# Two FFN projections of a hybrid decoder trunk as seven half-size block products instead of eight

## Chip, cores and metric

One NeuronCore of a Trainium2 chip. The metric is the device time of one execution in microseconds (us), the median of three runs.

## The reference

A decoder trunk of two layers on x of 1024 positions by 1024 features, float32. Layer 0 mixes with a state-space model and gated linear attention, layer 1 with an xLSTM matrix memory. After each mixer, and after each feed-forward block, the result is normalised and added to x. What the change concerns is the feed-forward block (FFN) that stands behind each mixer:

```python
def conv_ffn(h, w_up, conv_w, conv_b, w_down):          # h: 1024 x 1024
    g, u = jnp.split(h @ w_up, 2, axis=-1)              # w_up: 1024 x 5632
    g = causal_dwconv(g, conv_w, conv_b)                # width 3 along the sequence
    return ((jax.nn.gelu(g, approximate=True) * u) @ w_down)   # w_down: 2816 x 1024
x = x + rms_norm(mix, ln_mix_post[layer])
h = rms_norm(x, ln_ffn_pre[layer])
x = x + rms_norm(conv_ffn(h, ...), ln_ffn_post[layer])
```

## The kernel before

All large products run in a reduced-precision float format (fp32r). Each float32 operand is cut into a high part (ScalarE copy, `wh`, `hh`, `mh`) and a low part (VectorE subtraction x minus high, `wl`, `hl`, `ml`) by `cut` (L86 is the helper through which every vector operation is recorded), and `mm3` (L102) issues three matmuls for each product: high by high and the two mixed ones. A matmul has 128 rows of weights and streams 512 columns.

The order of the work on every engine is the order in which the program writes it. Weights come through one `Stream`: SyncE (SP) loads a 128x1024 float32 tile (`wr`, three buffers, 512 KB), then it is cut into `wh` and `wl` (three buffers each). `next()` hands out the next weight tile, and `advance(2)` in the middle of a tile's matmuls issues the cut of the tile two further on.

The sequence is done in two halves of 512 positions. `ffn` runs `ffn_half` for each half. A half takes 22 column tiles of g and u in two groups of 11: `proj` multiplies one 1024x128 column tile by the half's hT (24 matmuls), g is copied from PSUM to `gs`, GpSimd (POOL) does the first tap of the convolution, VectorE the other two, ScalarE the gelu, VectorE multiplies by u from PSUM, and the result is cut into `mh`, `ml` and stays in SBUF. After each group `down` multiplies the 11 tiles by the rows of `w_down`, into four PSUM banks for each half of the columns. Each weight is so loaded and cut twice, once for each half.

What stands between: `norms` adds two tasks, `postnorm` (scale, multiply by the gain, add x on POOL, sum of squares on ScalarE, store x) and `prenorm` (scale, transpose on TensorE, cut into hT). Tasks are generators on lanes; `tick`, called in every `mm3`, advances a lane when the planner's clock `now`, to which each matmul adds 4 ns plus its columns at 2.4 GHz, has passed its due time. So the norm of one half is spread between the matmuls of the other: half 1 of the mixer's output is normalised while `ffn_half` 0 runs, and half 1 of the FFN while the next stage's half 0 runs. `finish(task)` issues what is left of a task at once, without matmuls between.

Of the kernel before, what the change touches and what calls it, by code (L numbers as in the profile page):

```python
# [24 lines left out]

class Stream:
# [4 lines left out]
    def __init__(self, k, units):  # L31
        self.k, self.units = k, units
        self.raw, self.hl = {}, {}
        self.n_dma = self.n_cut = self.i = 0

    def _load(self):
        ap = self.units[self.n_dma]
        t = self.k.wpool.tile(list(ap.shape), F32, tag="wr", name="wr", bufs=self.RAW)
        self.k.nc.sync.dma_start(out=t, in_=ap)
        self.raw[self.n_dma] = t  # L40
        self.n_dma += 1

    def _cut(self):
        r = self.raw.pop(self.n_cut)
# [3 lines left out]
        self.hl[self.n_cut] = (h, l)  # L48
        self.n_cut += 1

    def advance(self, ahead):
        n = len(self.units)
        while self.n_dma < min(self.RAW, n):
            self._load()
        while self.n_cut < min(self.i + ahead, n):
            while self.n_dma < min(self.n_cut + self.RAW - 1, n):
                self._load()
            self._cut()

    def start(self):  # L60
        self._load()
# [29 lines left out]
class Products:  # L91
# [56 lines left out]
class Trunk:  # L148
    def __init__(self, tc, ins, out):
# [3 lines left out]
        self.inside, self.g_free, self.n_bank = False, False, 0  # L153
# [136 lines left out]
    def h_pair(self, shape):  # L290
        return [self.hpool.tile(shape, F32R, tag=t, name=t, bufs=8) for t in ("hh", "hl")]
# [10 lines left out]
    def prenorm(self, xt, ss, gain, layer, dst, slack, late=None):  # L302
# [11 lines left out]
        yield slack  # L314
        pend = None
# [15 lines left out]
    def norm_loads(self, src, half, gain, layer, before):  # L331
# [3 lines left out]
        xt = self.x_tiles()  # L335
# [7 lines left out]
    def norms(self, loads, half, y, ss, nxt):  # L343
# [3 lines left out]
        t1 = self.add(self.postnorm(xt, gb, s2, half, y, ss))  # L347
        if nxt is None:
            return None, t1, t1
        dst = self.h_slices()  # L350
        return dst, self.add(self.prenorm(xt, s2, nxt[0], nxt[1], dst, 4000)), t1
# [8 lines left out]
    def last_rows(self, xt, half, y, y2, ss):  # L360
# [3 lines left out]
        for t in (3, 0, 1, 2):  # L364
            r0 = half * HT + t * 128
            for n in range(2):
                c = slice(n * 512, (n + 1) * 512)
                o, x, r = (y2[t] if n else y[t][:, c]), xt[t][:, c], rs[:, t : t + 1]
# [7 lines left out]
    def postnorm(self, xt, gb, s2, half, y, ss):  # L376
        nc = self.nc
        rs = self.post_scale(ss)
        yield 2500

        def done(t):
            r0 = half * HT + t * 128
            nc.sync.dma_start(out=(self.out if s2 is None else self.xd)[r0 : r0 + 128], in_=xt[t])
            if s2 is not None:
                self.square_sum(xt, y[t], s2, t)

        for t in range(4):
            nc.vector.scalar_tensor_tensor(out=y[t], in0=y[t], scalar=rs[:, t : t + 1], in1=gb, op0=ALU.mult, op1=ALU.mult)
            nc.gpsimd.tensor_tensor(out=xt[t], in0=xt[t], in1=y[t], op=ALU.add)
# [6 lines left out]

    def ffn_units(self, layer):
        wu, wd = self.a["ffn_w_up"][layer], self.a["ffn_w_down"][layer]
        units = []
        for _ in range(2):  # L400
            for grp in range(2):
                for j in range(grp * HALF, (grp + 1) * HALF):
                    for base in (0, FFN):
                        c0 = base + j * 128
                        units.append(wu[:, c0 : c0 + 128].rearrange("(k p) c -> p k c", p=128))
                units += self.down_units(wd, list(range(grp * HALF, (grp + 1) * HALF)))
        return units

    def down_units(self, w, kts):
        units = []  # L410
        for n in range(2):
            i = 0
            while i < len(kts):
# [3 lines left out]
                    w[k0 * 128 : (k0 + m) * 128, n * 512 : (n + 1) * 512].rearrange("(k p) c -> p k c", p=128)  # L417
# [14 lines left out]
    def down(self, src, y, ss, add, before=(), late=None, final=None):  # L432

# [4 lines left out]
        for n in range(2):  # L438
            acc = [self.bank([128, HT]) for _ in range(4)]
            i = 0  # L440
            while i < len(src):
                if late and (n or final) and got is None and i >= len(src) - 4:
                    got = late()
# [18 lines left out]
            for t in range(4):  # L462
# [10 lines left out]
                if final:  # L473
                    eng = nc.vector if n and t > 1 else nc.gpsimd
                    eng.tensor_tensor(out=final[t] if n else o, in0=o, in1=got[1][:, n * 512 : (n + 1) * 512], op=ALU.mult)
# [5 lines left out]
    def ffn_half(self, layer, src, half, hT, before, nxt):  # L481
        nc = self.nc
        if half == 0:
            self.halo = self.fpool.tile([128, NF, 2], F32, tag="halo", name="halo", bufs=1)
        y, ss, final = None, self.sums(), None
        for grp in range(2):
            mids = []
            for j in range(grp * HALF, (grp + 1) * HALF):
                pg = self.proj(hT)
                gs = self.fpool.tile([128, HT + 2], F32, tag="gs", name="gs", bufs=2)  # L490
                tt = self.fpool.tile([128, HT], F32, tag="tt", name="tt", bufs=2)
                if half == 0:
                    nc.gpsimd.memset(gs[:, 0:2], 0.0)
                else:
                    nc.gpsimd.tensor_copy(gs[:, 0:2], self.halo[:, j])
                nc.scalar.activation(out=gs[:, 2:], in_=pg, func=AF.Copy)
                if half == 0:
                    nc.gpsimd.tensor_copy(self.halo[:, j], gs[:, HT : HT + 2])
                w = [self.par("ffn_conv_w", (layer * 3 + i) * NF + j) for i in range(3)]
                nc.gpsimd.tensor_scalar(  # L500
                    out=tt, in0=gs[:, 2:], scalar1=w[2], scalar2=self.par("ffn_conv_b", layer * NF + j),
                    op0=ALU.mult, op1=ALU.add,
                )
                for i in (1, 0):
                    nc.vector.scalar_tensor_tensor(
                        out=tt, in0=gs[:, i : i + HT], scalar=w[i], in1=tt, op0=ALU.mult, op1=ALU.add
                    )
                nc.scalar.activation(out=tt, in_=tt, func=AF.Gelu_apprx_tanh)
                pu = self.proj(hT)
                nc.vector.tensor_tensor(out=tt, in0=pu, in1=tt, op=ALU.mult)  # L510
                h = self.fpool.tile([128, HT], F32R, tag="mh", name="mh", bufs=HALF)
                l = self.fpool.tile([128, HT], F32R, tag="ml", name="ml", bufs=HALF)
                self.cut(h, l, tt)
                mids.append((h, l))
            late = (lambda: self.norm_loads(src, half, self.a["ln_ffn_post"], layer, before)) if grp else None
            if grp and half and nxt is None:
                h, l = (self.hpool.tile([128, 2, HT], F32, tag=t, name="fin", bufs=8) for t in ("hh", "hl"))
                final = [h[:, 0], h[:, 1], l[:, 0], l[:, 1]]
            y, loads = self.down(mids, y, ss if grp else None, grp == 1, before, late, final)
        if final:  # L520
            self.last_rows(loads[0], half, y, final, ss)
            return None
        return self.norms(loads, half, y, ss, nxt)

    def ffn(self, layer, src, hT, nxt):

        outs = []
        for half in range(2):
            self.finish(hT[half][1])
            before = [h[1] for h in hT + outs]  # L530
            outs.append(self.ffn_half(layer, src, half, hT[half][0], before, nxt))
# [3 lines left out]
    def even_units(self):  # L535
        w = self.a["ev_w_in"][0]

        def col(c0, n=128):
            return w[:, c0 : c0 + n].rearrange("(k p) c -> p k c", p=128)

        units = [col(c * 128) for c in range(4)]
        for _ in range(2):
# [3 lines left out]
            units += [w[k * 256 : (k + 1) * 256, 1024:1536].rearrange("(k p) c -> p k c", p=128) for k in range(4)]  # L546
            units += [col(1536 + c * 128) for c in range(4)]
        wg = self.a["s5_w_glu"][0]
        units += [wg[:, c * 128 : (c + 1) * 128].rearrange("(k p) c -> p k c", p=128) for _ in range(2) for c in range(4)]
# [744 lines left out]
    def layer0(self):  # L1294
# [4 lines left out]
        with sbuf_pool(tc, "mix") as self.mix, ExitStack() as self.s5_scope:  # L1299
# [49 lines left out]
            self.finish(gla1)  # L1349
        outs.append(self.mixer_out(1, x, s1 + self.gla_out[1], outs[0]))  # L1350
        return outs

    def mixer_out(self, half, x, src, other):
# [3 lines left out]
        return self.norms(loads, half, y, ss, ("ln_ffn_pre", 0))  # L1357
# [4 lines left out]
    def od_in_units(self):  # L1362
        w = self.a["od_w_in"][0]
        return [
            w[:, c * 128 : (c + 1) * 128].rearrange("(k p) c -> p k c", p=128) for _ in range(2) for c in range(32)
# [493 lines left out]
    def od_out_units(self):  # L1859
        w = self.a["od_w_out"][0]  # L1860
        units = [w[k * 128 : (k + 1) * 128].rearrange("(o p) c -> p o c", o=1) for k in range(self.NT)]
# [10 lines left out]
    def c_cut(self, raw, mids):  # L1872

        if mids:
            out = []
            for k in range(2):
                h = self.fpool.tile([128, HT], F32R, tag="mh", name="mh", bufs=HALF)
# [148 lines left out]
```

## Time and profile before

| | us |
|---|---|
| median of 3 runs | 2862.56 (2861.71 to 2865.48) |
| the profiled execution | 2865.5 |
| its span | 2863.8 |
| TensorE busy in the span | 2752.7 (96%) |
| VectorE, ScalarE, GpSimd busy | 1477.5, 1093.3, 489.1 |
| FFN of layer 0 (484.2 to 1244.5) | 760.3 |
| FFN of layer 1 (2118.5 to 2848.8) | 730.3 |

Busy time of a matmul is its time from start to modelled end; matmuls overlap, so their pitch (start to start) is what counts. An FFN stretch runs from its first projection matmul to the last matmul of `down`.

### The profile page before, as it was taken

The numbers are of one execution on the slowest core, as the hardware profiler recorded it, in microseconds if no ns is written. First come the engines' busy times: TensorE is split into PE (matmuls) and PEld (weight loads), VectorE is DVE, ScalarE is ACT, GpSimd is POOL, SyncE is SP. The second block draws the span as 40 slices with busy tenths as digits, with TensorE's granted clock in tenths as the row PEclk, the third lists the DMA queues.
The fourth block names the chain that finished last, engine by engine and source line by source line (L and its number), as shares of the span: only waits on it lengthen the run. The fifth ranks groups of instructions, "written<-read, shape, count | busy, mean of one in ns | idle before, by whom it ended". The sixth has DMA issues, their size and how long they took to land. (4 is left out here: it accounts for less than half of the span.)

```text
span 2863.8 us, 35476 instructions
## 1 busy us (share of the span) xinstructions
PE 2752.7 (96%) x13630; PEld 2289.7 (80%) x13630; DVE 1477.5 (52%) x2190; ACT 1093.3 (38%) x1717; POOL 489.1 (17%) x747
## 2 busy tenths in 40 slices
PE   6899998999999999999999999999999999999997
PEld 5677676788887888878788799998878888878886
DVE  7567554633435534457257367764546344353343
ACT  4233743432333323345345544443434233232332
POOL 2832002210002000020000035550111000110001
PEclk9999999999999999999999999999999999999999
DMA  4544435333334333355445534435443233342333
GB/s 122 163 130 139 139 129 143 112 103 106 94 105 140 103 96 96 99 183 154 143 142 160 166 114 142 134 106 214 168 147 100 96 94 96 129 125 98 101 93 113
DMA packets 457589, 360.69 MB, mean 126 GB/s; under 512 B 56750, under 2 KB 388104, under 8 KB 457292
## 3 DMA queue, kind: packets, MB, share of 16 engines
q1 hardware_dynamic: 418172, 323.23, 36.8%
q10 hardware_dynamic: 39248, 35.20, 3.6%
q8 instruction: 107, 1.75, 0.2%
q14 instruction: 62, 0.51, 0.1%
HBM read 291.05 MB, written 65.22 MB: 124 GB/s over the span
## 5 line engine op out<-in xcount | busy, mean ns | idle before, releaser
L86 DVE TENSOR_TENSOR wl<-wr,wh 128x1024 fp32r<-128x1024 f32 (+2 forms) x419 | 513.2, 1225 | 764.6 <-ACT wh L86 748.6
L102 PE MATMUL ps<-hh,wh 128*128 128x512 f32 (+1 forms) x2040 | 809.5, 397 | 5.1 <-ACT wh L86 5.1
L102 PE MATMUL ps<-hh,wl 128*128 128x512 f32 (+1 forms) x2040 | 801.0, 393 | 10.0 <-DVE wl L86 8.3
L102 PE MATMUL ps<-hl,wh 128*128 128x512 f32 (+1 forms) x2040 | 800.2, 392 | 0.0
L86 ACT ACTIVATE wh<-wr 128x1024 fp32r<-128x1024 f32 (+1 forms) x422 | 431.7, 1023 | 441.5 <-PE ps L102 355.5
L102 PEld LDWEIGHTS ps<-hh,wl 128*128 128x128 f32 (+1 forms) x2040 | 385.0, 189 | 97.7 <-DVE wl L86 12.6
L102 PEld LDWEIGHTS ps<-hh,wh 128*128 128x128 f32 (+1 forms) x2040 | 385.4, 189 | 93.5 <-ACT wh L86 8.1
L102 PEld LDWEIGHTS ps<-hl,wh 128*128 128x128 f32 (+1 forms) x2040 | 385.2, 189 | 78.9
L102 PE MATMUL ps<-wh,mh 128*128 128x512 f32 x730 | 285.6, 391 | 0.1
L102 PE MATMUL ps<-wl,mh 128*128 128x512 f32 x730 | 284.2, 389 | 0.8 <-DVE wl L86 0.8
L102 PE MATMUL ps<-wh,ml 128*128 128x512 f32 x730 | 284.2, 389 | 0.0
L86 DVE SCALAR_TENSOR_TENSOR tt<-gs,par_t,tt 128x512 f32<-128x512 f32 x176 | 132.9, 755 | 243.4 <-POOL tt L86 155.8
L86 POOL TENSOR_SCALAR tt<-gs,par_t 128x512 f32<-128x512 f32 x88 | 73.3, 833 | 511.7 <-ACT gs L86 511.7
L102 PEld LDWEIGHTS ps<-wl,mh 128*128 128x128 f32 x730 | 137.1, 188 | 29.2 <-DVE wl L86 1.1
L102 PEld LDWEIGHTS ps<-wh,mh 128*128 128x128 f32 x730 | 137.1, 188 | 28.5 <-ACT wh L86 0.5
L102 PEld LDWEIGHTS ps<-wh,ml 128*128 128x128 f32 x730 | 137.0, 188 | 28.5
L86 ACT ACTIVATE tt<-tt 128x512 f32<-128x512 f32 x88 | 55.6, 632 | 254.6 <-DVE tt L86 254.6
L102 PE MATMUL ps<-wh,hh 128*128 128x512 f32 x346 | 141.9, 410 | 9.2 <-DVE y L86 5.0
L102 PE MATMUL ps<-wl,hh 128*128 128x512 f32 x346 | 137.4, 397 | 1.5 <-DVE wl L86 1.5
L102 PE MATMUL ps<-wh,hl 128*128 128x512 f32 x346 | 137.0, 396 | 0.0
L86 ACT ACTIVATE mh<-tt 128x512 fp32r<-128x512 f32 x88 | 55.7, 632 | 170.0 <-DVE tt L86 170.0
L86 ACT ACTIVATE gs<-ps 128x512 f32<-128x512 f32 x77 | 46.1, 598 | 168.6 <-PE ps L102 168.5
(394 smaller groups left out, 3866.7 us busy)
## 6 DMA issues: line engine op xcount, KB each, us to landing
wr<-in_ffn_w_up_dram SPq DMA_DIRECT2D x176, 512.0 KB, 3.7
wr<-in_ffn_w_down_dram SPq DMA_DIRECT2D x80, 512.0 KB, 3.5
wr<-in_od_w_in_dram SPq DMA_DIRECT2D x64, 512.0 KB, 3.9
wr<-in_od_w_out_dram SPq DMA_DIRECT2D x32, 512.0 KB, 4.5
wr<-in_ev_w_in_dram SPq DMA_DIRECT2D x28, 512.0 KB, 5.1
xd<-x SPq DMA_DIRECT2D x24, 512.0 KB, 4.0
x<-xd SPq DMA_DIRECT2D x24, 512.0 KB, 6.1
wr<-in_ev_w_out_dram SPq DMA_DIRECT2D x16, 512.0 KB, 4.6
```

The lines of the kernel that those rows point to most:

```text
L86: return f(*args, **kw)
L102: self.eng.matmul(out=out, lhsT=lhsT, rhs=rhs, start=start, stop=stop)
```

## The change

The FFN works on both halves of the sequence at once, and halves all three dimensions of a product: two halves of the positions, two of the inner dimension, and a pair of output columns (g and u tile in the up projection, the two 512-column halves in the down projection). Seven block products with sums of blocks replace eight.

Up: for a pair of weight tiles a (g) and b (u), four tiles are cut: a, then a after POOL has replaced its halves by sums, then b likewise, then a half-size difference d. POOL does four 128x512 sums for a pair. The activations come as six blocks: 11 and 21 are half 0, and T1, T2, T3, T4, 22 are made from half 1 and half 0 by the new task `prenorm_blocks`. VectorE adds the products from PSUM into g and u in SBUF. The gated result goes to DRAM (`md`, 2816x1024), stored by SP.

Down: seven passes over 11 inner tiles, in jobs of two tiles (24 matmuls). Source blocks are loaded from `md` and weight blocks from `w_down`, both by SP. Where a pass wants a sum or difference of two blocks, POOL makes it, one 128x1024 operation for each job; then source and weights are cut. POOL makes both sums in passes 2, 4 and 6 (counted from 0), and one in passes 0, 1, 3 and 5. Each pass adds its four banks into one or two of the four quarters of the result.

`ffn` first finishes the norm tasks of both halves. The stream loads up to three units ahead; the planner's clock adds 14 ns instead of 4 ns per matmul.

```diff
-        self.now += 4 + n / 2.4 * (1 if rhs.dtype == F32R else 4)
+        self.now += 14 + n / 2.4 * (1 if rhs.dtype == F32R else 4)
...
+    def prenorm_blocks(self, xt, ss, gain, layer, base, out):
...
+        for c in range(4):
+            ps = []
+            for ct in (c, c + 4):
+                p = self.bank([128, 4, 128])
+                for t in range(4):
+                    nc.tensor.transpose(p[:, t], xt[t][:, ct * 128 : (ct + 1) * 128], self.ident)
+                ps.append(p.rearrange("p a b -> p (a b)"))
...
+            V.scalar_tensor_tensor(out=t12[:, 0], in0=ps[0], scalar=g[0], in1=h1, op0=ALU.mult, op1=ALU.subtract)
+            nc.scalar.activation(out=b[:, 0], in_=ps[0], func=AF.Copy, scale=g[0])
+            nc.scalar.activation(out=b[:, 1], in_=ps[1], func=AF.Copy, scale=g[1])
+            V.tensor_tensor(out=t12[:, 0], in0=t12[:, 0], in1=l1, op=ALU.subtract)
+            G.tensor_tensor(out=t34[:, 0], in0=b[:, 1], in1=b[:, 0], op=ALU.subtract)
...
+            V.tensor_tensor(out=t12[:, 1], in0=b[:, 1], in1=t12[:, 0], op=ALU.subtract)
+            V.tensor_tensor(out=t34[:, 1], in0=t12[:, 1], in1=h2, op=ALU.subtract)
+            G.tensor_tensor(out=t34[:, 1], in0=t34[:, 1], in1=l2, op=ALU.subtract)
+            h, l = pair()
+            self.cut(h, l, t12)
...
+            self.cut(h22[:, c % 2], l22[:, c % 2], b[:, 1])
...
+            self.cut(h, l, t34)
...
+        def sums(k, s):
+            G = k.nc.gpsimd
+            k.ws.live["wq"] += 1
+            s["d"] = k.ws.raw([128, 4, 128], "wq")
+            (a1, a2), (b1, b2) = ((s[n][:, 0:4], s[n][:, 4:8]) for n in "ab")
+            G.tensor_tensor(out=s["d"], in0=a1, in1=b1, op=ALU.subtract)
+            G.tensor_tensor(out=b1, in0=b1, in1=b2, op=ALU.add)
+            G.tensor_tensor(out=a1, in0=b1, in1=a1, op=ALU.subtract)
+            G.tensor_tensor(out=a2, in0=a2, in1=a1, op=ALU.subtract)
+            return s["a"]
...
+    def up_pair(self, B, g, u, late=None):
...
+        w = self.ws.next()
+        p = product(w, 0, B["11"])
+        nc.scalar.activation(out=u[:, lo], in_=p, func=AF.Copy)
+        acc(g[:, lo], u[:, lo], product(w, 1, B["21"]))
+        if late:
+            late()
+        wa, wb = self.ws.next(), None
+        acc(u[:, lo], u[:, lo], product(wa, 0, B["T2"]))
+        wb = self.ws.next()
+        acc(u[:, hi], u[:, lo], product(wb, 0, B["T1"]))
+        acc(u[:, lo], u[:, lo], product(wb, 1, B["T4"]), sub)
+        acc(g[:, hi], u[:, hi], product(wa, 1, B["22"]))
+        p = product(self.ws.next(), 0, B["T3"])
+        acc(u[:, hi], u[:, hi], p)
+        acc(u[:, lo], u[:, lo], p)
...
+    PASSES = (
+        (("11",), ("12", "-", "22"), (((0, 1), "="), ((1, 1), "="))),
+        (("11", "+", "12"), ("22",), (((0, 1), "+"), ((0, 0), "=-"))),
+        (("11", "+", "22"), ("11", "+", "22"), (((0, 0), "+"), ((1, 1), "+"))),
+        (("22",), ("21", "-", "11"), (((0, 0), "+"), ((1, 0), "="))),
+        (("12", "-", "22"), ("21", "+", "22"), (((0, 0), "+"),)),
+        (("21", "+", "22"), ("11",), (((1, 0), "+"), ((1, 1), "-"))),
+        (("21", "-", "11"), ("11", "+", "12"), (((1, 1), "+"),)),
+    )
...
     def ffn(self, layer, src, hT, nxt):
...
+        self.finish(hT[0][1])
+        B = {"11": hT[0][0][:4], "21": hT[0][0][4:]}
+        self.finish(hT[1][1])
+        B |= hT[1][0]
...
+        i, tt, v = pend
+        nc.vector.tensor_tensor(out=tt, in0=tt, in1=v, op=ALU.mult)
+        nc.sync.dma_start(out=self.md[i * 128 : (i + 1) * 128], in_=tt)
...
+        self.back(y, ss, after)
         return outs
```

In `up_pair`, `product` issues 12 matmuls on half of a weight tile and calls `advance(2)` after the sixth. The gate of a pair (convolution on POOL and VectorE, gelu on ScalarE) is written behind its seventh product, and its multiplication by u behind the next pair's second product. `back` issues, in the middle of each job, the cut of the weights two jobs on and the sum and cut of the sources of the next job; it moves a pass's four banks out after the pass's last matmul. During pass 5 the `postnorm` of half 0 runs, in pass 6 its `prenorm`.

## Rows read from the trace of the kernel before

**Rows 1.** The page: the span, and busy time of each engine.
```profile
span 2863.8 us, 35476 instructions
...
PE 2752.7 (96%) x13630; PEld 2289.7 (80%) x13630; DVE 1477.5 (52%) x2190; ACT 1093.3 (38%) x1717; POOL 489.1 (17%) x747
```

**Rows 2.** Windows: the two FFN stretches (length, busy us and count, granted clock, DMA share, GB/s).
```profile
484.20:1244.50 760.30, 752.62 (x3409) 621.98 (x3408) 339.94 (x392) 258.23 (x374) 87.69 (x149) 0.99 0.36 108
2118.50:2848.80 730.30, 725.26 (x3200) 598.05 (x3199) 324.17 (x360) 236.21 (x325) 74.52 (x127) 1.00 0.34 106
```

**Rows 3.** Timeline of TensorE in `down` (start, duration, operation); three matmuls from row to row.
```profile
839.76 0.39 PE L102 MATMUL ps<-wh,mh 128*128 128x512 f32 x1
...
840.44 0.39 PE L102 MATMUL ps<-wh,mh 128*128 128x512 f32 x1
```

**Rows 4.** Groups by form, whole span (count, busy us, mean ns, idle before).
```profile
L86 DVE TENSOR_TENSOR wl<-wr,wh 128x1024 fp32r<-128x1024 f32 x393 | 495.6, 1261 | 701.2 <-ACT wh L86 685.2 <-DMA so<-so 8.8 <-PE ps L102 6.3
L86 ACT ACTIVATE wh<-wr 128x1024 fp32r<-128x1024 f32 x396 | 416.0, 1050 | 377.1 <-PE ps L102 292.5 <-issue 18.6 <-DMA wr<-in_od_w_out_dram 14.4
...
L86 DVE SCALAR_TENSOR_TENSOR tt<-gs,par_t,tt 128x512 f32<-128x512 f32 x176 | 132.9, 755 | 243.4 <-POOL tt L86 155.8 <-POOL gs L86 84.3
L86 POOL TENSOR_SCALAR tt<-gs,par_t 128x512 f32<-128x512 f32 x88 | 73.3, 833 | 511.7 <-ACT gs L86 511.7
...
L86 DVE TENSOR_TENSOR tt<-ps,tt 128x512 f32<-128x512 f32 x88 | 60.1, 683 | 1.6 <-PE ps L102 1.6
...
L86 ACT ACTIVATE y<-x 128x1024 f32<-128x1024 f32 x24 | 25.4, 1058 | 48.4 <-POOL x L86 45.6 <-POOL xm L86 2.8
...
L86 DVE TENSOR_SCALAR x<-x,rs 128x1024 f32<-128x1024 f32 x28 | 20.9, 791 | 0.8 <-POOL rs L86 0.8
...
L86 POOL TENSOR_TENSOR ys<-cs,pi 128x512 f32<-128x512 f32 x8 | 9.2, 1152 | 0.4
```

**Rows 5.** Timeline of VectorE (DVE) and POOL during a `postnorm`, by time.
```profile
892.93 1.27 DVE L86 SCALAR_TENSOR_TENSOR y<-y,rsp,gb 128x1024 f32<-128x1024 f32 x1
894.12 0.68 DVE L86 TENSOR_TENSOR tt<-ps,tt 128x512 f32<-128x512 f32 x1
894.28 2.40 POOL L86 TENSOR_TENSOR x<-x,y 128x1024 f32<-128x1024 f32 x1 [2.36 <-DVE y L86]
...
898.51 2.35 POOL L86 TENSOR_TENSOR x<-x,y 128x1024 f32<-128x1024 f32 x1 [1.82 <-DVE y L86]
898.85 3.09 DVE L86 TENSOR_TENSOR wl<-wr,wh 128x1024 fp32r<-128x1024 f32 x1 [0.42 <-ACT wh L86]
```

**Rows 6.** Timeline: a one-input POOL operation beside a VectorE cut.
```profile
934.39 1.23 DVE L86 TENSOR_TENSOR wl<-wr,wh 128x1024 fp32r<-128x1024 f32 x1
935.16 1.11 POOL L86 TENSOR_SCALAR tt<-gs,par_t 128x512 f32<-128x512 f32 x1 [11.02 <-ACT gs L86]
```

**Rows 7.** Timeline where the mixer of layer 1 ends and the FFN begins.
```profile
2118.31 0.39 PE L102 MATMUL ps<-hh,wh 128*128 128x512 f32 x1
...
2119.47 0.63 ACT L86 ACTIVATE junk<-y 128x512 f32<-128x512 f32 x1
...
2120.67 1.01 POOL L86 TENSOR_TENSOR rsp<-ms,mhalf 128x4 f32<-128x4 f32 x1 [69.94 <-DVE ms L86]
```

**Rows 8.** Timeline of TensorE: eight transposes of a `prenorm`.
```profile
471.92 1.32 PE L106 MATMUL ps<-ident,x 128*128 128x128 f32 x8 [0.25 <-DVE hl L86]
```

**Rows 9.** The page's DMA issues: count, KB each, median us from issue to landing.
```profile
wr<-in_ffn_w_up_dram SPq DMA_DIRECT2D x176, 512.0 KB, 3.7
wr<-in_ffn_w_down_dram SPq DMA_DIRECT2D x80, 512.0 KB, 3.5
```

**Rows 10.** Windows of two short stretches in layer 0, columns as in rows 2.
```profile
455.00:466.00 11.00, 10.21 (x33) 8.19 (x34) 6.30 (x9) 4.90 (x10) 0.00 (x0) 0.70 0.16 47
...
476.00:484.20 8.20, 8.20 (x38) 6.79 (x37) 0.17 (x1) 0.00 (x0) 0.00 (x0) 1.00 0.97 335
```

**Rows 11.** Timeline of TensorE: the wait ahead of the first stretch of rows 10.
```profile
455.79 0.80 PE L102 MATMUL ps<-wh,hh 128*128 128x512 f32 x1 [3.99 <-DVE y L86]
```

More of the change, by code (lines that the diff above doesn't have):

```diff
@@ L314, in prenorm @@
         yield slack
+        while wait and not wait():
+            yield 500
+        if not dst:
+            dst += self.h_slices()
         pend = None
@@ L329, in prenorm, with norm_loads @@
             yield 600
-    def norm_loads(self, src, half, gain, layer, before):
+    def norm_loads(self, src, half, gain, layer, before, fresh=False):
         if before:
             self.finish(*before)
-        xt = self.x_tiles()
+        xt = [self.q_tile([128, D], F32, "xr") for _ in range(4)] if fresh else self.x_tiles()
         for t in range(4):
@@ new lines, in back_sources @@
+    def back_sources(self, src, n):
+        jobs = [(p, q) for p in range(len(self.PASSES)) for q in range(len(self.k_pairs(n)))]
+        self.b_src, self.b_n, self.b_raw, self.b_cut = src, n, {}, deque()
+        self.b_loads, self.b_jobs = deque(), deque(jobs)
+        seen = set()
+        for j, (p, q) in enumerate(jobs):
+            for name in self.PASSES[p][0][::2]:
+                if (name, q) not in seen:
+                    seen.add((name, q))
+                    self.b_loads.append((j, name, q))
+        self.b_done = 0
@@ new lines, in back_ahead @@
+    def back_ahead(self, upto):
+        while self.b_jobs and self.b_done <= upto:
+            p, q = self.b_jobs.popleft()
+            self.back_load(self.b_done + 2)
+            a = self.PASSES[p][0]
+            r = self.b_raw[a[0], q]
+            if len(a) > 1:
+                t = self.q_tile(list(r.shape), F32, "bsum")
+                self.nc.gpsimd.tensor_tensor(
+                    out=t, in0=r, in1=self.b_raw[a[2], q], op=ALU.add if a[1] == "+" else ALU.subtract
+                )
+                r = t
+            h, l = (self.q_tile(list(r.shape), F32R, name) for name in ("bh", "bl"))
+            self.cut(h, l, r)
+            self.b_cut.append((h, l))
+            self.b_done += 1
@@ L409, in down_units @@
+    def ffn_units(self, layer):
+        pairs = [(j * 128, FFN + j * 128) for j in range(NF)]
+        return self.up_units(self.a["ffn_w_up"][layer], pairs) + self.back_units(self.a["ffn_w_down"][layer], HALF)
     def down_units(self, w, kts):
@@ L479, in sums, with ffn @@
         return self.small.tile([128, 4, 2], F32, tag="ss", name="ss", bufs=2)
-    def ffn_half(self, layer, src, half, hT, before, nxt):
+    def ffn(self, layer, src, hT, nxt):
         nc = self.nc
[L483 to L493, printed above, removed]
-                else:
[L495 to L523, printed above, removed]
@@ L1872, in c_cut @@
     def c_cut(self, raw, mids):
[L1874 to L1877, printed above, removed]
[L1878 to L1882 removed]
+        h, l = self.q2_pair() if mids else self.h_pair([128, 2, HT])
         self.cut(h, l, raw)
```

327 lines of the change are left out of this document (262 added, 65 removed).

## The prediction

> **What bounds the kernel now.** I read the page first: TensorE is busy for 96% of the span [rows 1], so a matmul less should be time less. Then the windows of the two FFN stretches, 760.3 and 730.3 us, together 1490.6, with TensorE busy for 99% of them at a granted clock of 0.99 and 1.00, while VectorE is busy for about 45% and POOL for 10 to 12% [rows 2]. Then the timeline inside them: three matmuls take 0.68 us from start to start, so one takes 0.2267 us; the 0.39 us of a record is its latency [rows 3]. An FFN has 22 x 2 x 2 x 24 = 2112 matmuls in `proj` and 22 x 16 x 3 = 1056 in `down`. For both layers 6336 x 0.2267 = 1436.4 us, and 54 us of the 1490.6 are something else (30 us more in layer 0 than in layer 1, most of it TensorE work for the next layer and a second set of transposes). The reader should see that TensorE is the bound here because everything else has room and is spread evenly. The groups by form [rows 4] and two close looks at VectorE beside POOL [rows 5, 6] then give what the new work costs.
>
> **The change part by part. Removed:** seven products for eight leave 5544 matmuls: 22 x 84 = 1848 and 7 x 132 = 924 for each layer. 792 x 0.2267 = 179.5 us go, all of it on the path. 5544 x 0.2267 = 1256.8 us stay.
>
> **The shared door.** A 128x1024 addition on POOL alone takes 2.35 to 2.40 us [rows 5]. A VectorE cut that began 0.34 us after one took 3.09 us instead of 1.26 [rows 4, 5]: it ended 1.08 us after POOL did, so it stood still for the whole POOL operation. The VectorE product that reads PSUM kept its 0.68 us beside another such addition. So a VectorE operation with two SBUF inputs and a POOL sum add up. I count them as one queue. The change adds many POOL sums: four of 1.15 us (128x512 [rows 4]) for each pair, one or two of 2.37 us for each job of `down`. The one-input POOL operation took 1.11 us beside a cut instead of its usual 0.77 to 0.83 [rows 4, 6]; it waited, but there VectorE was first, and the rows show no cut that waited long for it. I count it as free of the lock. The Trainium skill (SBUF — State Buffer, Who interferes with whom) says that a VectorE instruction with two SBUF inputs contends with any GpSimd instruction that reads SBUF, and that whichever issues first blocks the other fully. By that the gate's POOL step, twice 0.77 = 1.54 us for 1024 columns, would hold the cut that follows a copy of 1.05 begun with it for 0.5 us in each pair, 21 us in all, and the sum would be 2949 instead of 2928.
>
> **The start of the FFN.** Every pair needs T1 to T4, and these need half 1. So `finish` now stands ahead of the first pair, and the norm of half 1, which was spread between matmuls, lies open on the path. From the last matmul of the mixer to the last sum of squares and the root: 2118.5 to 2121.7, 3.2 us [rows 7]. Four times multiply 1.27 and add 2.37, shutting each other out: 14.6 [rows 5]. A square, its reading and a second root: 1.06 + 0.3 + 1.2 = 2.6. Four scalings of 0.79: 3.2 [rows 4]. Eight transposes: 1.3 [rows 8]. Then four blocks of `prenorm_blocks`, in each on VectorE a step from PSUM 0.68, three of 0.63 (half of 1.26) and cuts of 1.26, 0.63 and 1.26, on POOL two of 1.15: 8.0 together, four times 32. Then the next weight cut, 1.26. Sum 58; T1's third matmul, the first to use that cut, stands 8.6 us into a pair anyway. TensorE loses 49 us; I take 48 for each layer, bounds 40 (POOL hidden) and 55.
>
> **A pair.** 84 matmuls are 19.04 us, a product 2.72. The weights of the fourth product (T1) are cut at the end of a long chain, because ScalarE and VectorE take their work in order. It starts where product 5 (T4) of the pair before frees a `wh` buffer: copy 1.05, cut 1.26, two POOL sums that may only then overwrite a 2.3, copy 1.05, cut 1.26, two additions from PSUM 1.36, one POOL sum of the pair after that gets in between 1.15, two convolution steps of 128x1024 at 1.27 each (the 128x512 one takes 0.755) 2.55, gelu 1.05, copy 1.05, cut 1.26 [rows 4, 5]. Together 15.3. TensorE wants the result five products and two matmuls later, after 14.05. So TensorE waits about 1.3 us in each pair, 21 pairs: 27 us for each layer. If VectorE gets the lock first it is 0.3 us (6); with POOL sums of 1.45 and steps of 1.5 it is 2.9 (61). The stores of `md` and the loads of a and b queue on SP, but the loads have two pairs of lead (38 us against 3.7 us [rows 9]); nothing.
>
> **From up to down.** SP stores the last gate before it issues the first source load. After the last matmul: two additions 1.4, convolution 2.55, gelu 1.05, product 1.25, store issue and load 4, copy and cut 2.3: 12.5, and the waits for POOL in the way. 14 us for each layer, 12 to 18. Before, 10 of the 11 tiles lay ready here.
>
> **Down.** A job is 24 matmuls, 5.44 us. Two cuts are 2.5 us and a POOL sum 2.37. With one sum 4.9, which fits; with both sums (passes 2, 4, 6) 7.2, which doesn't: 5.5 jobs cost 9.7 us too much, of which a lead of one job hides half: 15 us for three. In pass 5 the post-norm puts 14.6 us into the same queue with some 3 us of room: 9. At the six pass ends up to eight additions of 0.68 stand ahead of the next cuts, 5.4 + 2.5 against a lead of 5.44: 16. Sum 40 for each layer, bounds 20 and 70. Loads peak at three half megabytes in 5.44 us, 290 GB/s; a stretch with 335 GB/s is there [rows 10], so they fit.
>
> **The clock.** After 4.0 us without work [rows 11] the granted clock was 0.70 over 11 us [rows 10]: 6.6 us at half of 2.4 GHz, 3.3 us lost. The new idle times at the FFN's start, before `down` and at some pass ends are as long. I take 8 us for each layer, 3 to 15.
>
> **Sum.** 48 + 27 + 14 + 40 + 8 = 137 for each layer. FFN after: 1256.8 + 25 (layer 0's other work) + 274 = 1555.8, against 1490.6: +65 us. The profiled execution (2865.5, of which 1.7 lie outside the span) is 2.9 above the median, so the forecast is 2862.6 + 65 = **2928 us**. Outside the FFN the new planner clock and earlier loads shift lane work by a tenth of a microsecond or so for each ten matmuls; TensorE stands idle there for 1373 - 1275 = 98 us [rows 1, 2], of which I let a tenth move either way: 0, bounds -10 and +10.
>
> **The rivals.** *The saved matmuls win.* If POOL's sums fall into VectorE's gaps, in `prenorm_blocks`, in the pair's chain and in the passes with two sums, the low bounds hold: 40 + 6 + 12 + 20 + 3 = 81 for each layer, 1256.8 + 25 + 162 = 1444, -47 us, about 2816. It decides at 104 for each layer, where the sum is zero. For it: POOL and VectorE are busy for little of the FFN now [rows 2], and order decides who waits. Against: with the low bounds taken everywhere, the open norm of 48 us alone still eats half of a layer's 90 us. *A pair waits for the later buffer.* The `wh` buffer for the next pair's first tile could be the one that product 6 frees, not product 5: 2.7 us more for each pair, 42 times: +113, 3041 us. Nothing in the trace tells which; the earlier release is the natural one. *No change.* The losses are between the cases and cancel the gain, within 0.2% (about what a measurement of this kernel can tell from no change). That the change doesn't leave the matmuls out is excluded by the counts.
>
> **How the numbers follow.** Forecast 0.60 (slower), later buffer 0.08 (slower), matmuls win 0.27 (faster), no change 0.05. So faster 0.27, same 0.05, slower 0.68. The range leaves the later buffer and the end of the fast case out: 2825 to 3000. The forecast's own range is 2875 to 2990, by the bounds of pairs and `down`.
>
> **What would show it.** Right: TensorE idle for 45 to 50 us between the mixer and the third product, with VectorE and POOL alternating; 20.3 us from pair to pair, with TensorE waiting on VectorE's `wl` in the fourth product; cuts of over 2 us wherever POOL's sums run; passes 2, 4 and 6 of `down` longer than 30 us; a granted clock of 0.5 at these places. Wrong: pairs of 19.0 us, or passes of 30 us, would mean that the sums hide, and the time falls below 2862.

## The result, and the profile after

The changed kernel takes 3008.66 us (median of 4 runs, 3005.14 to 3013.14) against 2862.72 for the kernel before (4 runs too): a ratio of 1.0509, 95% interval 1.0491 to 1.0527. The direction was forecast; the size, 2928, was not, and the range ended at 3000.

The page after, answering to [rows 1]: the span, and busy time of each engine.

```profile
span 3008.7 us, 34282 instructions
...
PE 2649.7 (88%) x12838; PEld 2172.3 (72%) x12838; DVE 1882.6 (63%) x2417; ACT 1073.1 (36%) x1632; POOL 1064.0 (35%) x883
...
PEclk9999996999999899899999999999969999989987
```

792 matmuls are gone, TensorE's busy time fell by 103 us, and the span grew by 145. The last row is the granted clock in 40 slices: all nines before; now it dips where each FFN begins, and ahead of and in each `down`. The windows of the two FFN stretches (columns as in [rows 2]):

```profile
469.70:1317.10 847.40, 706.27 (x3013) 566.58 (x3013) 532.01 (x506) 246.29 (x331) 364.96 (x213) 0.91 0.35 111
2194.40:2993.10 798.70, 677.87 (x2805) 539.69 (x2804) 532.34 (x476) 226.21 (x284) 355.52 (x190) 0.92 0.35 112
```

They grew by 87 and 68 us. The mixer of layer 0 ends 14.5 us earlier, the stage between the FFNs takes 3 more. The forecast had 1555.8 us for both stretches; they take 1646.1. What layer 1 loses beyond 2772 x 0.2267 = 628.4 us splits so:

| layer 1, us lost | forecast | measured |
|---|---|---|
| open norm | 48 | 51.6 |
| 22 pairs | 27 | 21 |
| from up to down | 14 | 17 |
| `down`, with the clock (40 + 8) | 48 | 80 |
| sum | 137 | 170 |

**Open norm.** Timeline of TensorE where the FFN of layer 1 begins; in brackets the wait ahead of an instruction and what ended it:

```profile
2214.63 0.47 PE L138 MATMUL ps<-ident,x 128*128 128x128 f32 x1 [20.11 <-DVE x L118]
...
2239.21 0.80 PE L134 MATMUL ps<-hh,wh 128*128 128x512 f32 x1 [6.09 <-ACT hh L118]
...
2248.25 0.80 PE L134 MATMUL ps<-hh,wh 128*128 128x512 f32 x1 [6.09 <-ACT hh L118]
2254.58 0.79 PE L134 MATMUL ps<-hh,wl 128*128 128x512 f32 x1 [0.23 <-DVE wl L118]
```

Twenty us up to the first transpose, then a block every 9.04 us, with T1's third matmul as its end. The whole is near the forecast, its parts are not: up to the transposes 23.6 us were forecast, and 8.0 for a block. In each block VectorE also stands still for 0.67 and 0.57 us until ScalarE has made a copy, which the forecast didn't count.

**Pairs.** Two steps of TensorE, one pair apart:

```profile
2336.27 0.50 PE L134 MATMUL ps<-hh,wl 128*128 128x512 f32 x1 [0.36 <-DVE wl L118]
2355.97 0.50 PE L134 MATMUL ps<-hh,wl 128*128 128x512 f32 x1 [0.37 <-DVE wl L118]
```

19.70 us from pair to pair, 0.66 over the matmuls instead of 1.3, and the wait stands where it was expected, at the weights of T1. That makes 14 of the 21 us; the rest is lost in the first pair and at the last. In layer 0 it is otherwise. ScalarE's gelu comes once in a pair; here it is in layer 0:

```profile
671.65 1.06 ACT L118 ACTIVATE xs<-xs 128x1024 f32<-128x1024 f32 x1 [4.78 <-issue]
700.18 1.06 ACT L118 ACTIVATE xs<-xs 128x1024 f32<-128x1024 f32 x1 [5.05 <-DVE xs L118]
719.88 1.06 ACT L118 ACTIVATE xs<-xs 128x1024 f32<-128x1024 f32 x1 [5.05 <-DVE xs L118]
```

28.5 us, then 19.7. The first six gelus of layer 0 stand 27 to 31 us apart, 43 us in all over 19.7; there `od_prep`, the other work of layer 0, puts its small products between the pairs, and TensorE stands in front of them (the first wait lies in the open norm, ahead of the first pair):

```profile
525.06 0.69 PE L138 MATMUL ps<-ident,bd 128*128 128x128 f32 x2 [27.15 <-POOL bd L118]
588.27 0.80 PE L134 MATMUL ps<-bt,bt 128*128 128x128 f32 x2 [7.46 <-ACT bt L118]
```

**Down.** 285.7 and 289.4 us, from first to last matmul, for 209.5 us of matmuls. The largest single wait, in layer 1 ahead of pass 6, with POOL, ScalarE and VectorE by time:

```profile
2952.84 3.70 POOL L118 TENSOR_TENSOR x<-x,gb 128x512 f32<-128x512 f32 x3 [18.50 <-DMA gb<-in_ln_ffn_post_dram]
2957.72 2.34 POOL L118 TENSOR_TENSOR wr<-wr,wq 128x1024 f32<-128x1024 f32 x1
2960.01 2.34 POOL L118 TENSOR_TENSOR bsum<-braw 128x1024 f32<-128x1024 f32 x1
2962.39 1.06 ACT L118 ACTIVATE bh<-bsum 128x1024 fp32r<-128x1024 f32 x1 [1.25 <-POOL bsum L118]
2963.48 3.25 DVE L118 TENSOR_TENSOR bl<-bsum,bh 128x1024 fp32r<-128x1024 f32 x1
2963.50 0.79 PE L134 MATMUL ps<-wh,bh 128*128 128x512 f32 x1 [16.45 <-ACT bh L118]
2965.61 3.35 POOL L118 TENSOR_TENSOR bsum<-braw 128x1024 f32<-128x1024 f32 x1
2966.77 3.28 DVE L118 TENSOR_TENSOR wl<-wr,wh 128x1024 fp32r<-128x1024 f32 x1
```

POOL waits for the gain `gb` to land, and the sums of pass 6 stand behind it. The last rows show the lock: every sum and every cut takes 3.3 us, one shut out until the other ends. The weights' cuts in this `down`, as a group:

```profile
L118 DVE TENSOR_TENSOR wl<-wr,wh 128x1024 fp32r<-128x1024 f32 x33 | 65.3, 1979 | 79.6 <-ACT wh L118 79.6
```

They take 1.98 us on average instead of 1.26 [rows 4]. The longest pass is 5, where the post-norm of half 0 runs, with 53.5 us for 29.9 us of matmuls:

```profile
2899.84 6.61 POOL L118 TENSOR_TENSOR y<-xr,y 128x1024 f32<-128x1024 f32 x2 [3.68 <-DVE y L118]
2900.82 3.40 DVE L118 TENSOR_TENSOR wl<-wr,wh 128x1024 fp32r<-128x1024 f32 x1
2906.41 2.33 POOL L118 TENSOR_TENSOR bsum<-braw 128x1024 f32<-128x1024 f32 x1
2909.89 0.74 PE L134 MATMUL ps<-wh,bh 128*128 128x512 f32 x1 [3.89 <-ACT bh L118]
```

The next job's sum stands on POOL behind two additions of the post-norm, which the lock makes 3.3 us each. These wait for VectorE's multiplications, which stand behind the cut of the sum before. So the steps close a ring: from sum to sum it takes 12.6 us (2906.41 to 2918.99), where a job's matmuls take 5.44. Behind such waits TensorE runs at the lower of its two clocks, 1.2 GHz, for a while: 0.43 us from matmul to matmul instead of 0.2267, and a granted clock of 0.89 for the whole of `down` (0.60 in the open norm, 2194.4 to 2254.6).

```profile
2967.38 0.63 PE L134 MATMUL ps<-wh,bh 128*128 128x512 f32 x1
2967.81 0.63 PE L134 MATMUL ps<-wl,bh 128*128 128x512 f32 x1
...
2703.50:2993.10 289.60, 236.79 (x924) 186.21 (x924) 176.30 (x127) 88.91 (x116) 157.84 (x65) 0.89 0.48 163
```

Of the 80 us, 57 are lost at matmuls with a wait ahead of them and 23 at others that follow each other too slowly.

### The profile page after: what moved, and what is told of

Its sections match the earlier page's. It is cut to its first block, busy times and chain, and to the rows that moved or that the text cites. A ratio compares the mean times of both kernels' runs of the same rounds, so it can differ in the third digit from the quotient of the medians.

```text
span 3008.7 us, 34282 instructions
## 1 busy us (share of the span) xinstructions
PE 2649.7 (88%) x12838; PEld 2172.3 (72%) x12838; DVE 1882.6 (63%) x2417; ACT 1073.1 (36%) x1632; POOL 1064.0 (35%) x883
## 5 line engine op out<-in xcount | busy, mean ns | idle before, releaser
L118 DVE TENSOR_TENSOR wl<-wr,wh 128x1024 fp32r<-128x1024 f32 (+1 forms) x319 | 434.2, 1361 | 613.9 <-ACT wh L118 601.6
L134 PE MATMUL ps<-hh,wh 128*128 128x512 f32 x1876 | 749.9, 400 | 20.5 <-ACT hh L118 13.6
L134 PE MATMUL ps<-hh,wl 128*128 128x512 f32 x1876 | 743.7, 396 | 17.7 <-DVE wl L118 15.9
L134 PE MATMUL ps<-hl,wh 128*128 128x512 f32 x1876 | 740.5, 395 | 3.1 <-DVE hl L118 3.1
L134 PEld LDWEIGHTS ps<-hh,wl 128*128 128x128 f32 x1876 | 356.2, 190 | 110.5 <-DVE wl L118 31.9
L134 PEld LDWEIGHTS ps<-hh,wh 128*128 128x128 f32 x1876 | 356.7, 190 | 105.0 <-ACT hh L118 15.5
L134 PEld LDWEIGHTS ps<-hl,wh 128*128 128x128 f32 x1876 | 356.8, 190 | 77.9 <-DVE hl L118 4.4
L134 PE MATMUL ps<-wh,bh 128*128 128x512 f32 x572 | 239.8, 419 | 79.2 <-ACT bh L118 79.2
L134 PE MATMUL ps<-wh,bl 128*128 128x512 f32 x572 | 242.4, 424 | 54.2 <-DVE bl L118 53.7
L134 PE MATMUL ps<-wl,bh 128*128 128x512 f32 x572 | 235.8, 412 | 0.0
```

Of the source, the lines that this page charges most:

```text
L118: return f(*args, **kw)
```

## The experiments

**1. Down's sums on VectorE.**

```diff
-                k.nc.gpsimd.tensor_tensor(out=s["a"], in0=s["a"], in1=s["c"], op=op)
+                k.nc.vector.tensor_tensor(out=s["a"], in0=s["a"], in1=s["c"], op=op)
...
-                self.nc.gpsimd.tensor_tensor(
+                self.nc.vector.tensor_tensor(
```

> The sums of blocks in the down projection (weights and sources) move from POOL to VectorE; nothing else changes. Theory (the sums and VectorE's cuts shut each other out, and POOL needs 2.4 us for what VectorE does in 1.23): a job with two sums then takes VectorE 2.5 + 2.5 = 5.0 us, less than the 5.44 us of its matmuls, the cuts go back to about 1.2 us, and in layer 1 the sums of pass 6 no longer stand on POOL behind the multiplication that waits for gb (16.45 us). Down falls from 289.8 and 285.7 us to 240 to 260 each, the whole to about 2940 (2915 to 2960). Rival (down is long because of what happens at pass ends: drains, loads, clock): VectorE only gets more work, down stays within 10 us, and the whole stays at 2990 to 3020.

3009.94 us (ratio to the kernel before 1.0513, 1.0497 to 1.0529): no gain, and down takes 295.1 and 286.7. The total is the rival's, but its reason isn't. VectorE and ScalarE in a pass with two sums:

```profile
2862.02 1.22 DVE L118 TENSOR_TENSOR wr<-wr,wq 128x1024 f32<-128x1024 f32 x1
2863.36 1.06 ACT L118 ACTIVATE wh<-wr 128x1024 fp32r<-128x1024 f32 x1 [7.29 <-DVE wr L118]
2864.45 1.22 DVE L118 TENSOR_TENSOR wl<-wr,wh 128x1024 fp32r<-128x1024 f32 x1 [1.21 <-ACT wh L118]
2865.59 1.22 DVE L118 TENSOR_TENSOR bsum<-braw 128x1024 f32<-128x1024 f32 x1
2866.90 1.06 ACT L118 ACTIVATE bh<-bsum 128x1024 fp32r<-128x1024 f32 x1 [2.49 <-DVE bsum L118]
2867.99 1.23 DVE L118 TENSOR_TENSOR bl<-bsum,bh 128x1024 fp32r<-128x1024 f32 x1 [1.18 <-ACT bh L118]
2869.13 1.22 DVE L118 TENSOR_TENSOR wr<-wr,wq 128x1024 f32<-128x1024 f32 x1
```

Cuts are back at 1.22 us, so the lock is gone. But the cut is written right behind its sum, and VectorE keeps its order: it stands still for 1.2 us at each copy of ScalarE. That is 7.1 us for a job, by chance what the prediction counted for the locked queue (7.2). That the total is the same is chance too: layer 1, where pass 6's sums no longer wait for `gb`, gains 3 us in `down` and layer 0 loses 9; ahead of `down` both gain some us. My theory had counted busy times where a row of steps has waits in it.

**2. Down with eight products.** The seven passes become eight of one block each, without sums (`PASSES` and the passes at which the quarters are done; the rest stays).

```diff
+        (("11",), ("12",), (((0, 1), "="),)),
+        (("12",), ("22",), (((0, 1), "+"),)),
+        (("11",), ("11",), (((0, 0), "="),)),
...
```

> The down projection with eight plain block products in eight passes, same loads, cuts and drains, no sums at all: 132 matmuls more for each layer, 29.9 us. Theory (the sums cost down more than the matmul saved): down takes 1056 x 0.2267 = 239 us plus 15 to 25 for pass ends and clock, 255 to 265 each against 289.8 and 285.7, the whole 2945 to 2965. Rival (pass ends, late loads and the post-norm in the passes are the cost, and there is now one pass more): down 315 to 325 each, the whole about 3070.

2946.48 us (1.029, 1.0275 to 1.0305). Down takes 261.6 and 258.4 with 132 matmuls more: as the theory said. The sums cost about 60 us more than the matmuls that they saved, for both layers.

**3. The gate preparation four pairs later.**

```diff
-                self.add(self.od_prep(), 1)
...
+            if layer == 0 and j == 4:
+                self.add(self.od_prep(), 1)
```

> The preparation of the next layer's gates (od_prep: transposes and small products on TensorE) is begun four pairs later in layer 0's FFN; nothing is left out. Theory (in layer 0 these small products are put between the first pairs, while POOL, ScalarE and VectorE still lag from the open norm, and TensorE stands in front of them): the waits of 27.15 us at 525.06 and 7.46 at 588.27 shrink, the first pairs look like those of layer 1, FFN 0 falls by 20 to 35 us, the whole to about 2982 (2972 to 2990). Rival (the pairs wait for the norm chain anyway, the small products only stand in front of the same wait): 3000 to 3012.

3008.41 us (1.0509, 1.0491 to 1.0526): nothing gained. The first six intervals between gelus are 19.7 to 20.2 now, but the next six 27 to 29. The lag of the norm isn't the cause; a pair without slack pays for this work wherever it stands.

**4. The gain multiplication inside pass 6.**

```diff
                 if nxt is None:
-                    final_gain(0)
+                    loads[2] = self.add(gain_task())
```

> In layer 1 the multiplication of the second half's first columns by the gain gb is issued some 20 us into pass 6, instead of at the end of pass 5, where POOL waits for gb to land; nothing is left out. Theory (pass 6's sums stand on POOL behind that wait): the idle time of 16.45 us ahead of pass 6's third job falls to 2 or 3 us, with some half-clock time behind it, the whole to about 2993 (2988 to 2998). Rival (pass 6's sums would be late anyway, since their weight blocks are loaded late and POOL needs 4.8 us for a job): at most 5 us, 3004 or more.

2999.82 us (1.0476, 1.0459 to 1.0493), 9 less. Down of layer 1 goes from 289.4 to 273.3 in the profile, and the wait of 16.45 is gone; a wait of 3.60 for VectorE's `bl` stands at 2944.38 instead. So the wait was the cause of those 16 us, as in the theory; the total lies just above the theory's range, between it and the rival's.

**5 and 6. The sums one job ahead of their cuts**, on VectorE and on POOL. Edit 6 is this alone; 5 adds the two lines of experiment 1.

```diff
         self.n_cut += 1
+        n = self.n_cut
+        if n < min(self.n_dma, len(self.units)) and self.units[n].done == ("a", "c"):
+            self.made[n] = self.units[n].make(self.k, self.units[n].state)
...
             self.b_done += 1
+            if self.b_done > 1:
+                self.back_sum(self.b_done)
```

> Down's sums on VectorE as in the first experiment, but each sum is issued right behind the cut before it, one job ahead of its own cut; nothing is left out. There a job with two sums took 7.1 us: sum, wait for ScalarE's copy, subtraction, sum, wait, subtraction (2862.02 to 2869.13). Theory (the row sum, copy, subtraction is what is too long, because VectorE keeps its order and stands still during each copy): the sums fall into those gaps, a job takes VectorE about 4.6 us, less than 5.44, and down falls from 286.7 and 295.1 to 250 to 268 each; the whole 2940 to 2965. Rival (VectorE's pass ends, the post-norm and the loads are the cost): 280 or more each, the whole above 2985.

> The same reordering with the sums left on POOL. Theory (POOL's sums and VectorE's cuts shut each other out): 2 x 2.35 + 2 x 1.14 = 7.0 us for a job with two sums, whatever the order, so the passes with two sums stay as long as they are; down stays at 275 to 292 each, the whole 2985 to 3012. Rival (only the row sum, copy, subtraction is too long, and POOL works beside VectorE when the sum is early): down 250 to 268 each, the whole 2940 to 2965, as with VectorE.

On VectorE 2947.41 us (1.0297, 1.0279 to 1.0314), down 261.5 and 257.3; on POOL 2983.95 (1.0422, 1.0406 to 1.0437), down 275.3 and 274.0. Both are the theory's, the second at the lower edge of its range. On VectorE, in a pass with two sums:

```profile
2821.41 1.22 DVE L123 TENSOR_TENSOR bsum<-braw 128x1024 f32<-128x1024 f32 x1
2822.55 1.22 DVE L123 TENSOR_TENSOR wl<-wr,wh 128x1024 fp32r<-128x1024 f32 x1
2822.73 1.06 ACT L123 ACTIVATE bh<-bsum 128x1024 fp32r<-128x1024 f32 x1 [1.21 <-DVE bsum L123]
2823.68 1.22 DVE L123 TENSOR_TENSOR wr<-wr,wq 128x1024 f32<-128x1024 f32 x1
2824.82 1.22 DVE L123 TENSOR_TENSOR bl<-bsum,bh 128x1024 fp32r<-128x1024 f32 x1
2825.96 1.22 DVE L123 TENSOR_TENSOR bsum<-braw 128x1024 f32<-128x1024 f32 x1
```

From sum to sum 4.55 us, no gap, and ScalarE copies beside it. On POOL with the same order:

```profile
2847.97 3.31 POOL L123 TENSOR_TENSOR bsum<-braw 128x1024 f32<-128x1024 f32 x1 [2.30 <-DVE bl L123]
2848.95 3.42 DVE L123 TENSOR_TENSOR bl<-bsum,bh 128x1024 fp32r<-128x1024 f32 x1
```

Both 3.3 to 3.4: the lock. So there are two costs: the order of the steps (25 us for both layers, with POOL) and the lock with what else stands on POOL, the wait for `gb` among it (37 more). The lock's part doesn't show while the order stands, which is why experiment 1 moved nothing.

**7. The planner's pace in the kernel before.**

```diff
-        self.now += 4 + n / 2.4 * (1 if rhs.dtype == F32R else 4)
+        self.now += 14 + n / 2.4 * (1 if rhs.dtype == F32R else 4)
```

> The kernel before with the planner's clock of the changed kernel (14 ns for a matmul instead of 4) and nothing else. In the changed kernel the mixer of layer 0 ends 14.5 us earlier. Theory (that comes from the pace): 2849 (2845 to 2854), the mixer ends at about 470. Rival (it comes from the loads that the stream issues further ahead, or from the weights' order): 2858 to 2868, the mixer ends at 484.

2861.4 us (0.9993, 0.9984 to 1.0002), no difference that can be measured. The mixer ends 6.4 us earlier in the profile (477.75), not 14.5. The theory falls; what gives the rest stays open. In the other runs of the changed order the mixer ends at 471.3 to 474.7, so up to 5 us of the 14.5 are spread from run to run.

**8. The order alone.** Both projections with eight products and no sums; the rest of the order stays.

```diff
+        one, two = B["11"] + B["21"], B["T1"] + B["22"]
+        w = self.ws.next()
+        nc.scalar.activation(out=g[:, lo], in_=product(w, one), func=AF.Copy)
+        nc.scalar.activation(out=g[:, hi], in_=product(w, two), func=AF.Copy)
...
```

> The changed kernel's order (both halves at once, the norms ahead of the first pair, the gated result through DRAM) with eight products in both projections and no sums anywhere. Worked out from the down with eight products (2946.5): up takes 22 x 12 x 0.2267 us more for each layer, 119.7 in all; the 0.66 us a pair waits in each pair, 29, goes, and the open norm has half the VectorE work for each of its four blocks, some 16 us less for each layer: about 3005 (2990 to 3020). Theory (up's seven products are worth their sums): 45 to 75 us slower than the down with eight products. Rival (up's sums cost as much as they save): 2935 to 2955.

2950.0 us (1.0304, 1.0288 to 1.032), the same as with up's seven products (2946.5): the rival. But not because the pairs cost as much. They take 21.78 us here (96 x 0.2267 = 21.76) against 19.70. Experiment 2 has the same `down`; against it the seven products save 44 us from the first gelu of layer 1 to its last. From the mixer's end to that first gelu they need 79.1 us instead of 53.7, since T1 to T4 must be made on VectorE and POOL: 25 us back. So in layer 1 up's seven products are worth some 19 us. In layer 0 it is 33 back for 19 saved, since pairs of 21.8 grow to only 24 to 27 with the gate preparation in them. The rest of the 2950, 87 us over the kernel before, is the order: the norms ahead of the pairs, the way through DRAM, the passes, the gate preparation; no run splits it.

**9. The gate preparation in the gap.**

```diff
-        yield 60000
+        yield 4000
```

(and the other waiting times of `od_prep` times 0.3)

> The changed kernel with the preparation of the next layer's gates begun at once and stepped at 0.3 of its waiting times, so that most of it is issued while the open norm leaves TensorE idle; nothing is left out. Moved by four pairs it had cost the same: the six pairs that hold it take 27 to 31 us instead of 19.7, some 45 us in all. Theory (the pairs have no slack, the open norm's gap has): nearly all pairs of layer 0 take 19.7, the gap grows by at most 15 us for the 24 products on POOL, the whole 2972 to 2988. Rival (POOL, ScalarE and VectorE are what the norm itself waits for, so the gap grows by what the pairs lose): 3000 to 3012.

2983.46 us (1.0421, 1.0403 to 1.0438), 25 less: the theory. Up to the 20th gelu, pairs of layer 0 take 19.7 us, and the largest wait in its gap is now 9.97 instead of 27.15. The pairs give 43 us and the gap takes 19 of it back (first gelu 108.4 us behind the mixer instead of 89.0), more than the 15 of the theory.

**10. The open norm's differences on VectorE**, in both layers; the planner goes on counting them for POOL, so its order stays.

```diff
-            G.tensor_tensor(out=t34[:, 0], in0=b[:, 1], in1=b[:, 0], op=ALU.subtract)
+            V.eng.tensor_tensor(out=t34[:, 0], in0=b[:, 1], in1=b[:, 0], op=ALU.subtract)
...
-            G.tensor_tensor(out=t34[:, 1], in0=t34[:, 1], in1=l2, op=ALU.subtract)
+            V.eng.tensor_tensor(out=t34[:, 1], in0=t34[:, 1], in1=l2, op=ALU.subtract)
```

> In the open norm the two 128x512 differences of each block that POOL makes (1.15 us each) move to VectorE (0.63); nothing is left out. The four blocks stand 9.05 us apart in layer 1. Theory (POOL and VectorE shut each other out there, so the times add): 2 x 0.52 us less for each block, 8.0 us apart, 8 us in all, about 3000. Rival (the block is a chain of steps that wait for each other, and POOL's share lies beside VectorE's): 9.0 or more apart, 3005 to 3013.

2998.05 us (1.0472, 1.0451 to 1.0493), 11 less. Two blocks of layer 1:

```profile
2232.17 0.80 PE L134 MATMUL ps<-hh,wh 128*128 128x512 f32 x1 [4.95 <-ACT hh L118]
...
2239.85 0.79 PE L134 MATMUL ps<-hh,wh 128*128 128x512 f32 x1 [4.95 <-ACT hh L118]
```

7.68 us apart instead of 9.04: the times add there, as in the theory, and the lock cost a little more than the theory counted (1.36 us for a block instead of 1.04).

**11. Up's sums on VectorE.**

```diff
-            G = k.nc.gpsimd
+            G = k.nc.vector
```

> Up's four sums for each pair on VectorE (0.63 us each) instead of POOL (1.3); nothing is left out. A pair takes 19.70 us, 0.66 more than its matmuls. Theory (the chain of copies, cuts and sums behind the fourth product sets the pair, and POOL's sums are part of it): 19.05 to 19.3 us from pair to pair, 10 to 28 us in all, 2980 to 2999. Rival (as in down, a sum ahead of the copy and the cut makes VectorE wait for ScalarE, which costs what POOL cost): 19.6 to 20.5, 3003 to 3040.

3177.04 us (1.1097, 1.1075 to 1.1119), 168 slower, worse than the rival's worst. Pairs of layer 1 take 24.2 us on average. VectorE, POOL and ScalarE, where a weight is cut, summed and copied again:

```profile
2489.59 1.23 DVE L118 TENSOR_TENSOR wl<-wr,wh 128x1024 fp32r<-128x1024 f32 x1 [4.79 <-ACT wh L118]
2490.73 1.40 DVE L118 TENSOR_TENSOR ys<-ys,ps 128x512 f32<-128x512 f32 x2
2492.65 0.69 DVE L118 TENSOR_TENSOR wq<-wr,wq 128x512 f32<-128x512 f32 x1
2492.83 1.58 POOL L118 TENSOR_SCALAR xs<-xs,par_t 128x1024 f32<-128x1024 f32 x1 [22.41 <-DVE xs L118]
2493.37 1.58 DVE L118 TENSOR_TENSOR wq<-wq 128x512 f32<-128x512 f32 x1
2496.50 1.06 ACT L118 ACTIVATE wh<-wr 128x1024 fp32r<-128x1024 f32 x1 [6.94 <-DVE wr L118]
```

From copy to copy (2488.49 to 2496.50) 8.0 us; with POOL it is 5.2 (2341.36 to 2346.54). On VectorE the sums stand behind additions that read TensorE's products, and all stages of the chain share one order. POOL's own queue was what kept them off it.

**12. Three repairs together** (5, 9 and 10).

> The changed kernel with three of the edits together: down's sums on VectorE one job ahead of their cuts (61 us less alone), the gate preparation in the gap of the open norm (25 less), the open norm's differences on VectorE (11 less). They lie in different stretches, so the theory (each cost is lost on TensorE's path in its own place) adds them: 3008.7 - 97 = 2912 (2902 to 2922). Rival (they share a cost: the gap that takes the gate preparation is shortened by the third, and a shorter down moves the next wait): 2925 to 2945. By either it stays slower than the kernel before, by 1.4% or more, since the open norm of layer 1, the way from up to down and the pass ends remain.

2916.45 us (1.0185, 1.0168 to 1.0202), 92 less of the 97: they add, nearly in full. The open norm of layer 1, both ways from up to down, and waits in `down` (258.9 us for 209.5) remain. The kernel before, with either pace, stays the fastest of all that were run.

## Why the prediction was wrong in size

The forecast is 80 us short. `down`, with the clock, makes 60 of it (32 in layer 1, 28 in layer 0) and layer 0's other work 24; the remaining terms and the stretches outside the FFN nearly cancel.

**Removed matmuls and open norm.** 792 are gone, as counted. The norm lost 51.6 us where 48 were forecast, and experiment 10 shows the lock there much as it was counted. That the sum came out is in part luck: 3 us too much up to the transposes stood against 1.0 too little in each of the four blocks, where VectorE waits for ScalarE.

**A pair.** The chain and its place were right, its size twice too high (0.66 us for 1.3). From ScalarE's copy behind T4 (2341.36) to the end of the cut for T1 (2355.92) it took 14.6 us instead of 15.3: the POOL sum of the next pair, which I had let in between VectorE's steps at 1.15, comes only behind that cut (2356.00).

```profile
2341.36 1.06 ACT L118 ACTIVATE wh<-wr 128x1024 fp32r<-128x1024 f32 x1 [5.41 <-PE ps L134]
2346.49 1.20 POOL L118 TENSOR_SCALAR xs<-xs,par_t 128x1024 f32<-128x1024 f32 x1
2347.63 1.23 DVE L118 TENSOR_TENSOR wl<-wr,wh 128x1024 fp32r<-128x1024 f32 x1 [2.03 <-ACT wh L118]
...
2354.69 1.23 DVE L118 TENSOR_TENSOR wl<-wq,wh 128x1024 fp32r<-128x1024 f32 x1 [2.12 <-ACT wh L118]
2356.00 1.29 POOL L118 TENSOR_TENSOR wq<-wr,wq 128x512 f32<-128x512 f32 x1 [8.32 <-DVE wl L118]
```

The later `wh` buffer (the rival with 3041) is excluded by the 19.70.

**Down.** This term failed: "Sum 40 for each layer", plus 8 for the clock. Together they measured 80 in layer 1 and 76 in layer 0. The lock itself was right: where sums and cuts meet they take 3.3 us each. Passes of layer 1 in us, for 29.9 us of matmuls each (passes 2, 4 and 6 have two sums, pass 5 the post-norm):

| pass | 0 | 1 | 2 | 3 | 4 | 5 | 6 |
|---|---|---|---|---|---|---|---|
| changed kernel | 32.7 | 35.3 | 42.9 | 37.0 | 35.8 | 53.5 | 52.4 |
| 1: sums on VectorE | 34.7 | 35.6 | 40.6 | 40.0 | 42.9 | 50.3 | 42.7 |
| 6: early, on POOL | 32.9 | 30.6 | 41.9 | 37.7 | 35.5 | 47.2 | 48.4 |
| 5: early, on VectorE | 32.4 | 31.0 | 38.6 | 36.1 | 35.7 | 43.9 | 39.9 |

Passes 2, 4 and 6 were to lose 5 us each ("of which a lead of one job hides half: 15 us for three") and 2.7 at the pass end. They lost 13, 6 and 22, and 16 of the 22 was a wait that I had put at nothing: the gain that POOL waited for with pass 6's sums behind it (experiment 4). Without it they are near the forecast. The step that failed is "In pass 5 the post-norm puts 14.6 us into the same queue with some 3 us of room: 9": with its pass end, pass 5 lost 24 us here and 28 in layer 0. The post-norm did not add its time to a queue with room. It closed the ring of 12.6 us, and no lead hides that, because each sum stands directly ahead of its cut. Without sums the same pass loses 8 or 9 us (experiment 2: 37.6 and 38.6 us). The forecast asked who waits for a wait on VectorE and not who stands behind one on POOL.

Experiments 6 and 5 take out the order, then the lock: 32 of the 80 go in layer 1 (289.4 to 257.3), 24 of the 76 in layer 0. For the 48 to 52 that remain no run shows more than the table. The clock was too small as well: "8 us for each layer" was to cover all of it, and in `down` alone it took some 23 and 26 us, since there are many waits and matmuls at 1.2 GHz behind each of the longer ones.

**Layer 0's other work.** "FFN after: 1256.8 + 25 (layer 0's other work)" took the 25 us over from before, where it lay between matmuls that had slack behind them. Layer 0 loses 49 us more than layer 1, where it was 30 before. The five long intervals are 43 of it, and experiment 9 gives 25 back by moving the work alone.

**Outside the FFN.** Forecast 0, -10 to +10; it was -14.5 and +3, so -11. The new pace alone does 6 of it and doesn't show in the total (experiment 7).

**The rivals.** "The saved matmuls win" needed the low bounds everywhere. In layer 1 of experiment 12, 46 us (51.6 less four times 1.36), 17, 15 and 50 are still lost, 128, where that rival needed 81 and 104 was the turning point. The rule of the Trainium skill (SBUF — State Buffer, Who interferes with whom) that a GpSimd instruction which reads SBUF blocks a two-input VectorE instruction, one input or not, would have added 21 us by the prediction's estimate. Experiment 11 shows that it holds: beside the one-input POOL step of 1.58 us a VectorE sum took 1.58 instead of 0.69. In the changed kernel that POOL step (2346.49, 1.20 us) ends as the cut begins (2347.63, 1.23), so the 21 us did not come.

## What to carry to other kernels

Fewer matmuls pay only where the engines that feed TensorE have slack in that stretch and in that order (up's pairs in layer 1 had it, and gained 19 us): here 180 us of matmuls were traded for 335 us of waits and lower clock (1646.1 - 1490.6 + 179.5), though VectorE was busy for only 63% of the time. Where a sum feeds a copy and a subtraction on two engines that keep their order, issue it a step ahead, and count the time of a row of steps, not their busy time. Before a task is made a barrier, look at what the program puts between matmuls later: work that was free beside slack is paid in full without it.

## What was not expected of the hardware

The lock works in both directions and adds nearly the whole of the other instruction: a 128x1024 cut of 1.22 us took up to 3.50 beside a POOL sum, and a POOL sum of 2.35 took up to 3.51 beside cuts. It doesn't always change hands after one instruction: in pass 5 of layer 1 of experiment 5 a POOL addition of the post-norm took 6.74 us (from 2857.23) while four VectorE instructions with two SBUF inputs ran one behind the other, and the fifth (from 2861.61) then took 3.43 instead of 1.28. The trace doesn't show why POOL wasn't let in sooner. And a fix that looks useless alone can pay behind another: moving the sums of `down` from POOL to VectorE gave nothing in the old order and 37 us with the sums a job ahead, which alone gave 25. In the up projection the same move cost 168 us.
